# Moving the decay matrices and the first convolution tap to ScalarE, and all weight splits to VectorE, in a hybrid SSD and mLSTM layer

## The chip, the cores and the metric

The kernel runs on one core of a Trainium2 chip, as one program. The metric is the device time of one execution in microseconds (us), the median of several runs; lower is better. Engines are named as in the profile: PE is TensorE, DVE is VectorE, ACT is ScalarE, POOL is GpSimd, SP is SyncE, whose queue issues most DMAs.

## The reference, cut to what matters

One decoder layer for 1024 tokens of width 1024, all in float32. A normalised and modulated input `h` goes through one wide projection. Its columns feed a Mamba-2 branch (SSD: 32 heads in 4 groups, chunks of 128 tokens) and an mLSTM branch (4 heads); both merge, and a SwiGLU feed-forward follows. The change concerns the causal convolution that both branches begin with, and the decay matrices of the SSD branch:

```python
proj = h @ w_in[l]
z, xbc, dt, qk, v, o, if_pre, gate_pre = split_sizes(proj, IN_SPLITS)
...
xbc = jax.nn.silu(causal_depthwise_conv(xbc, conv_w, conv_b))     # 4 taps, per channel
...
a_cs = jnp.cumsum(a, axis=-1)                 # a = dt * A, per head and chunk
decay = jnp.exp(segsum(a))                    # exp(a_cs[l] - a_cs[s]) where l >= s, else 0
cb = jnp.einsum('bclgn,bcsgn->bgcls', cm, bm)
y_diag = jnp.einsum('bgcls,bgrcls,bcsgrp->bclgrp', cb, decay, x)
```

## The kernel before

All large products run on PE in exact pairs of float32r numbers: an operand is split into a high and a low part, and three matmuls (high by high, high by low, low by high) of 128 x 512 make one product. `split` (line 120) makes such a pair of a weight tile `raw` of 128 x 1024: ACT casts the high part `wh` (line 123), and another engine subtracts to get the low part `wl` (line 124). That engine is `eng["l"]`: POOL until the end of the SSD stage, DVE from there on (`eng["l"] = V`, line 677). There are two buffers of `wl` and three of `wh`, so a split waits until PE has finished with an older tile.

The work lies in stages. A prologue (about 0 to 60 us) loads `x`, normalises it and makes the modulation vectors, where DVE reduces 16 weight tiles (line 155). The SSD stage (about 60 to 600 us) does 16 head pairs, `ssd_pair`, four to a group. The mLSTM stage (about 600 to 1530 us) does four heads and the gates. Phase B (from about 1530 us) has the branch projections, the merge and the feed-forward.

`conv_tile` (line 293) makes one convolved tile of 128 channels x 1024 tokens: `gemm` fills a PSUM bank for each half (512 tokens) with 24 matmuls (line 287), ACT copies each to SBUF (`cr`, line 298), DVE makes the first tap and the bias out of `cr` (line 305) and adds three taps (line 307), ACT takes a tanh (line 308), and DVE finishes the SiLU (line 309). `gemm` has two banks (`mm`): PE fills one while the other is read.

`ssd_pair` (line 449) takes one `conv_tile`, and for each half `q` a tile `ab` of two heads by four chunks of 128 x 128: a DMA brings the cumulative sums along the row, POOL subtracts those of the column (line 466), DVE takes the minimum with 0 (line 467), ACT the exponential (line 468), DVE multiplies by the masked product of B and C (line 470), and PE multiplies by the values (line 494). `ab` has two buffers. `z_gate` (line 511) multiplies a result by silu(z): ACT takes the tanh from the bank (line 521), DVE multiplies it by the same bank (line 522), POOL does two more products (lines 523 and 533).

Within an engine, instructions run in the order of its queue. That order is not the order of the source: the framework's scheduler sets it at build time, from its own model of how long each instruction takes (`schedule_with_timeline_sim=True`). So a change of an instruction's engine also moves its neighbours.

Of the kernel before, what the change touches and what calls it, by code (L numbers as in the profile page):

```python
# [15 lines left out]
P = 128  # L16
# [3 lines left out]
NCH = 8  # L20
L = 128
# [15 lines left out]
def hybrid_layer(ctx: ExitStack, tc: tile.TileContext, a: dict, out: bass.AP, dbg=None):  # L37
# [80 lines left out]
    eng = {"l": G}  # L118

    def split(raw):  # L120
        wh = wp.tile([P, 1024], F32R, name="wh", bufs=NWH)
        wl = wp.tile([P, 1024], F32R, name="wl", bufs=NWL)
        A.copy(wh, raw)  # L123
        eng["l"].tensor_tensor(wl, raw, f(wh), SUB)  # L124
        return wh, wl
# [67 lines left out]
    def to_feat(src, bank, k, w, b, hf):  # L193
        """Four token-major tiles -> one modulated feature tile (128 x 512)."""
        for t in range(4):
            T.transpose(bank[:, t * P:(t + 1) * P], src[t][:, k * P:(k + 1) * P], ident)
        A.activation(hf, bank, AF.Identity, scale=mod[:, w, k:k + 1], bias=mod[:, b, k:k + 1])
# [5 lines left out]
    # =========================================================== norm 1 and the first products, k by k  # L203
# [12 lines left out]
    NG = 40                                                # dt (32), i (4), f (4)  # L216
# [75 lines left out]
    # ---- projection + causal conv + silu, feature-major  # L292
    def conv_tile(col, cw, cb, ti, pre=None):
        dst = xf("xf")
        cr = crt("cr")

        def epi(hf, ps):
            A.copy(cr[:, halves(hf)], ps)

        if pre is None:  # L300
            gemm(w_in[:, col:col + P], epi)
        else:
            for hf in range(2):
                epi(hf, pre[:, hf])
        V.tensor_scalar(dst, cr, cw[:, 3, ti:ti + 1], cb[:, ti:ti + 1], MUL, ADD)
        for sh in (1, 2, 3):
            V.scalar_tensor_tensor(dst[:, sh:], cr[:, :S - sh], cw[:, 3 - sh, ti:ti + 1], dst[:, sh:], MUL, ADD)  # L307
        A.activation(cr, dst, AF.Tanh)
        V.scalar_tensor_tensor(dst, cr, 1.0, dst, ADD, MUL)
        return dst  # L310
# [10 lines left out]
    # ---- per-token gates, token-major: columns dt (0..31), i (32..35), f (36..39) of every chunk  # L321
# [40 lines left out]
    V.scalar_tensor_tensor(flat(sp_), flat(gt), 0.0, flat(q0), MAX, ADD)      # softplus  # L362
    V.tensor_tensor(e0, sp_, fac.unsqueeze(1).broadcast_to([P, NCH, NG]), MUL)  # dt * A, log_f
    pcum, ptot = sc_bank()[:, 0:320], sc_bank()[:, 0:320]
    T.matmul(pcum, lhsT=mask01, rhs=flat(e0), start=True, stop=True)       # per-chunk cumulative sums
    T.matmul(ptot, lhsT=ones, rhs=flat(e0), start=True, stop=True)         # per-chunk totals on every partition
# [16 lines left out]
    # mLSTM stabilisers: rows of log_i - b, their running maximum, the maxima carried over chunks  # L383
# [29 lines left out]
    V.tensor_tensor(chv(cmx), chv(cmx), minb, MAX)          # mx = max(m_in, running max)  # L413
    V.tensor_tensor(chv(tw), minb, chv(cmx), SUB)           # w_inter = exp(m_in - mx)
# [6 lines left out]
    A.activation(em_t, em_t, AF.Exp, scale=-1.0)            # exp(-m_t), m_t = b + mx  # L421
# [3 lines left out]
    A.activation(w_t, w_t, AF.Exp)                          # exp(g - m_new + log_i - b)  # L425

    # ---- SSD
    sqacc = cp.tile([P, S], F32, name="sqacc")

    def ssd_bc(g):  # L430
        """C (feature-major), the masked products of B and C, and B token-major, for all chunks of a group."""
        b = conv_tile(OFF_B + P * g, cw_s, cb_s, 16 + g, pre=psb if g == 0 else None)
        cc = conv_tile(OFF_C + P * g, cw_s, cb_s, 20 + g)
        cbm, bt = xf("cbm"), xf("bt")
        for q in range(2):
            ps = sc_bank()
            for c in range(4):
                sl = slice((4 * q + c) * L, (4 * q + c + 1) * L)
                T.matmul(ps[:, c * L:(c + 1) * L], lhsT=b[:, sl], rhs=cc[:, sl], start=True, stop=True)
            V.tensor_tensor(cbm[:, halves(q)].rearrange("p (c l) -> p c l", l=L), ps.rearrange("p (c l) -> p c l", l=L),  # L440
                            mask01.unsqueeze(1).broadcast_to([P, 4, L]), MUL)
            ps = sc_bank()
            for c in range(4):
                sl = slice((4 * q + c) * L, (4 * q + c + 1) * L)
                T.transpose(ps[:, c * L:(c + 1) * L], b[:, sl], ident)
            A.copy(bt[:, halves(q)], ps)
        return cc, cbm, bt

    def ssd_pair(g, j, grp):
        """Heads 8g+2j and 8g+2j+1, all chunks; head pairs lie on partitions 0..63 and 64..127 of the result."""  # L450
# [11 lines left out]
        for q in range(2):  # L462
            ab[q] = ap.tile([P, 2, 4, L], F32, name="ab", tag="t4", bufs=2)
            Q.dma_start(ab[q].rearrange("p h c l -> p h (c l)"), acs_d[h0:h0 + 2, halves(q)].unsqueeze(0).broadcast_to([P, 2, 512]))
            ta = acs_t[:, 4 * q:4 * q + 4, h0:h0 + 2].rearrange("p c h -> p h c")
            G.tensor_tensor(ab[q], ab[q], ta.unsqueeze(3).broadcast_to([P, 2, 4, L]), SUB)  # L466
            V.tensor_scalar(ab[q], ab[q], 0.0, None, MIN)
            A.activation(ab[q], ab[q], AF.Exp)
# [42 lines left out]
    def z_gate(r, Y=None):  # L511
        """u = Y * silu(z) and its share of the row sums of squares; Y comes from DRAM where it was put off."""
# [22 lines left out]
    # ---- mLSTM  # L535
# [6 lines left out]
    def ml_v(h):  # L542
        """Token-major: tile i holds the 512 columns of the chunks 2i and 2i + 1."""
        vt = [xf("vt") for _ in range(4)]
        for u in range(2):
# [6 lines left out]
            for i in range(4):  # L552
                ps = mm_bank().rearrange("p (c n) -> p c n", c=2)
                for c in range(2):
                    sl = slice((2 * i + c) * L, (2 * i + c + 1) * L)
                    lo, hi = (0, 1, 2, 3), (4, 5, 6, 7)
                    if i + c == 0:                         # the low parts of the weights come last ...
                        order = ((0, 0, lo), (1, 0, lo), (0, 1, lo), (0, 0, hi), (1, 0, hi), (0, 1, hi))
                    else:                                  # ... and are given up first
                        order = ((0, 1, lo), (0, 1, hi), (0, 0, lo), (1, 0, lo), (0, 0, hi), (1, 0, hi))  # L560
                    ops = [(x_, w_, k) for x_, w_, ks in order for k in ks]
                    for n, (x_, w_, k) in enumerate(ops):
                        T.matmul(ps[:, c], lhsT=hT[k][x_][:, sl], rhs=ws[k // 4][w_][:, k % 4], start=n == 0, stop=n == 23)  # L563
# [11 lines left out]
    def ml_scan(h, q, k, v):  # L575
        C = ap.tile([P, 2, 514], F32, name="C")
        CH = CL = None
        for c in range(NCH):
# [37 lines left out]
            # state  # L616
# [26 lines left out]
            # normaliser, per-head rms  # L643
# [33 lines left out]
    eng["l"] = V  # L677
    later = chain(mod_steps(2, mod_row, 0), mod_steps(3, mod_cols, 2), mod_steps(4, mod_cols, 3), mod_steps(5, mod_row, 1))
    q, k, v = ml_q(0), ml_k(0), ml_v(0)
    def ssd_rms():  # L680
        # ssd rms: rows of 1/rms broadcast over partitions, times the factors left out above
# [35 lines left out]
    # =========================================================== phase B  # L717
# [30 lines left out]
    def kouter(nk, load, mm):  # L748
        """Products k by k into eight banks; the last two k bank by bank, so that the banks end one after another."""
# [9 lines left out]
    def residual(yt, ss, src, bk, ahead=None):  # L759
        """yt = src + two banks; ss = 1 / rms of its rows."""  # L760
# [201 lines left out]
```

## Time and profile before

| | |
|---|---|
| runs | 2756.96, 2765.63, 2765.8 us; median 2765.63 us |
| profiled execution: span from its first to its last instruction | 2757.1 us |
| PE busy | 2663.9 us, 97% of the span |
| DVE busy | 1449.5 us, 53% |
| ACT busy | 876.6 us, 32% |
| POOL busy | 657.4 us, 24% |

The page gives the profiled execution's own time by its span alone, which is as long as the shortest run; the median of the runs is 8.5 us above it. Busy shares are means over the whole span: the stages have different limits, so the rows below go by stage.

### The profile page before, as it was taken

How to read it: one execution, taken by the hardware profiler on the slowest of the kernel's cores; microseconds unless marked ns; L12 is line 12 of the kernel's file. 1: busy time of each engine (PE TensorE's matmuls, PEld its weight loads, DVE VectorE, ACT ScalarE, POOL GpSimd, SP SyncE). 2: the span in 40 equal slices, each digit the busy share in tenths (PEclk: the TensorE clock that was granted, in tenths of full speed). 3: DMA queues.
4: the chain of work that ended last, by engine and by line, in shares of the span. 5: the costliest groups of instructions: out<-in, count | busy, mean ns of one | idle time of the engine just before them, and what ended most of it. 6: DMA issues, size and time to landing. Idle time of an engine off the chain costs nothing.

```text
span 2757.1 us, 34111 instructions
## 1 busy us (share of the span) xinstructions
PE 2663.9 (97%) x13543; PEld 2223.4 (81%) x13543; DVE 1449.5 (53%) x2033; ACT 876.6 (32%) x1355; POOL 657.4 (24%) x447
## 2 busy tenths in 40 slices
PE   5999988999999999999999999999999999999998
PEld 3878777879888988988988877787788888788886
DVE  8688876895742463254354245536543343433333
ACT  5332322232431333243243223323242221322222
POOL 4333353420210011011032011401411134311154
PEclk9999999999999999999999999999999999999999
DMA  6323231343344332123132455646343333433332
GB/s 196 104 90 116 87 120 62 112 130 115 112 135 143 93 115 87 60 71 100 52 114 93 162 183 165 210 146 194 123 145 99 95 107 98 153 99 92 102 128 92
DMA packets 297000, 323.78 MB, mean 117 GB/s; under 512 B 15584, under 2 KB 224832, under 8 KB 296840
## 3 DMA queue, kind: packets, MB, share of 16 engines
q1 hardware_dynamic: 289416, 296.43, 34.8%
q0 software_dynamic: 7424, 25.17, 2.5%
q8 instruction: 106, 1.74, 0.3%
q14 instruction: 54, 0.44, 0.1%
HBM read 274.59 MB, written 46.96 MB: 117 GB/s over the span
## 4 chain that ended last, share of the span: by engine, by line
PE 74%; DVE 4%; DMA 1%; issue 1%; POOL 0%; ACT 0%; DVEq 0%; POOLq 0%; SPq 0%; ACTq 0%
PE mm L287 22%; PE mm L888 17%; PE mm L563 7%; PE n L800 6%; PE n L840 6%; PE mm L800 3%; PE sc L800 3%; PE mm L840 3%; PE sc L840 3%; PE n L615 2%; PE n L633 1%; DVE wl L124 1%; DMA uk<-y_d 1%; PE sc L584 1%; PE sc L655 1%
## 5 line engine op out<-in xcount | busy, mean ns | idle before, releaser
L124 DVE TENSOR_TENSOR wl<-raw,wh 128x1024 fp32r<-128x1024 f32 x283 | 395.7, 1400 | 665.8 <-issue 161.6
L123 ACT CAST wh<-raw 128x1024 fp32r<-128x1024 f32 x316 | 332.2, 1051 | 961.1 <-POOL raw L140 217.7
L287 PE MATMUL mm<-hh,wh 128*128 128x512 f32 x1392 | 551.1, 396 | 9.9 <-DVE tz L522 8.9
L287 PE MATMUL mm<-hl,wh 128*128 128x512 f32 x1392 | 550.3, 395 | 0.0
L287 PE MATMUL mm<-hh,wl 128*128 128x512 f32 x1392 | 548.0, 394 | 0.0
L888 PE MATMUL mm<-h,wh 128*128 128x512 f32 x1408 | 435.6, 390 | 2.1 <-DVE th L892 2.1
L287 PEld LDWEIGHTS mm<-hh,wh 128*128 128x128 f32 x1392 | 262.9, 189 | 65.2 <-DVE tz L522 9.9
L888 PEld LDWEIGHTS mm<-h,wh 128*128 128x128 f32 x1408 | 264.8, 188 | 57.3 <-DVE th L892 2.6
L287 PEld LDWEIGHTS mm<-hh,wl 128*128 128x128 f32 x1392 | 262.6, 189 | 52.0 <-issue 0.9
L287 PEld LDWEIGHTS mm<-hl,wh 128*128 128x128 f32 x1392 | 263.0, 189 | 50.3 <-issue 0.5
L888 PE MATMUL mm<-h,wl 128*128 128x512 f32 x704 | 274.9, 390 | 0.5 <-DVE wl L124 0.5
L140 POOL TENSOR_TENSOR raw<-raw,gb 128x1024 f32<-128x1024 f32 x60 | 151.9, 2533 | 305.1 <-DMA raw<-in_w_out_dram 175.0
L307 DVE SCALAR_TENSOR_TENSOR xf<-cr,pk,xf 128x1023 f32<-128x1023 f32 (+2 forms) x120 | 180.4, 1506 | 1.7
L800 PE MATMUL n<-us,wh 128*128 128x512 f32 x512 | 161.9, 397 | 2.8 <-DVE am L818 2.8
L896 POOL TENSOR_TENSOR act<-th,act 128x512 fp32r<-128x512 f32 x44 | 69.8, 1587 | 373.1 <-ACT act L895 373.1
L888 PEld LDWEIGHTS mm<-h,wl 128*128 128x128 f32 x704 | 132.5, 188 | 28.8 <-DVE wl L124 1.4
L124 POOL TENSOR_TENSOR wl<-raw,wh 128x1024 fp32r<-128x1024 f32 x33 | 89.4, 2710 | 174.4 <-PE mm L287 129.1
L191 POOL TENSOR_TENSOR sm<-sm,mhalf 128x1 f32<-128x1 f32 x32 | 20.2, 630 | 418.0 <-DVE sm L190 418.0
L800 PEld LDWEIGHTS n<-us,wh 128*128 128x128 f32 x512 | 96.8, 189 | 27.1 <-DVE am L818 3.3
L840 PE MATMUL n<-wh,act 128*128 128x512 f32 x352 | 116.7, 393 | 0.0
L466 POOL TENSOR_TENSOR ab<-ab,gsum 128x1024 f32<-128x1024 f32 x32 | 68.9, 2152 | 145.4 <-DMA ab<-acs_d 135.2
L800 PE MATMUL n<-us,wl 128*128 128x512 f32 x256 | 101.7, 399 | 0.0
(295 smaller groups left out, 4180.8 us busy)
## 6 DMA issues: line engine op xcount, KB each, us to landing
raw<-in_w_in_dram SPq DMA_DIRECT2D x104, 512.0 KB, 3.8
raw<-in_w_ffn_in_dram SPq DMA_DIRECT2D x88, 512.0 KB, 3.7
raw<-in_w_ffn_out_dram SPq DMA_DIRECT2D x44, 512.0 KB, 3.4
raw<-in_w_ada_dram SPq DMA_DIRECT2D x40, 512.0 KB, 3.7
tg_d<-tz POOLq DMA_DIRECT2D x64, 256.0 KB, 2.9
ab<-acs_d SPq DMA_DIRECT2D x32, 512.0 KB, 3.8
raw<-in_w_branch_ssd_dram SPq DMA_DIRECT2D x32, 512.0 KB, 3.6
tgl<-tg_d SPq DMA_DIRECT2D x64, 256.0 KB, 2.9
```

Source lines behind the costliest of these rows:

```text
L123: A.copy(wh, raw)
L124: eng["l"].tensor_tensor(wl, raw, f(wh), SUB)
L140: G.tensor_tensor(raw, raw, gate, MUL)
L287: T.matmul(ps, lhsT=ww[:, k, :], rhs=xx[:, halves(hf)], start=n == 0, stop=n == 23)
L307: V.scalar_tensor_tensor(dst[:, sh:], cr[:, :S - sh], cw[:, 3 - sh, ti:ti + 1], dst[:, sh:], MUL, ADD)
L466: G.tensor_tensor(ab[q], ab[q], ta.unsqueeze(3).broadcast_to([P, 2, 4, L]), SUB)
L563: T.matmul(ps[:, c], lhsT=hT[k][x_][:, sl], rhs=ws[k // 4][w_][:, k % 4], start=n == 0, stop=n == 23)
L615: T.matmul(nv(i), lhsT=l_, rhs=r_, start=n == 0, stop=n == len(ops) - 1)
L800: T.matmul(bk[j], lhsT=l_[:, js], rhs=us[:, r_], start=first and n == 0, stop=last and n == 2)
L840: T.matmul(bk[i], lhsT=at[:, l_, tt * P:(tt + 1) * P], rhs=r_[:, halves(nh)], start=first and n == 0, stop=last and n == 2)
L888: T.matmul(ps, lhsT=ww[:, k, :], rhs=h2[k][:, r_], start=k == 0 and n == 0, stop=k == KD - 1 and n == 2)
L896: G.tensor_tensor(at[:, 1], th, f(at[:, 0]), SUB)
```

## The change

Three edits. The first: the low part of every weight split is made by DVE, in the prologue and the SSD stage too. The second: the first tap of a convolution, with its bias, is made by ACT straight from the PSUM bank, half by half, where DVE made it of the copy. The third: for the decay matrices, POOL's subtraction and DVE's minimum become one ACT function with a column of biases, `relu(t - a)` for each block of 128 x 128 (the column's sum t is one number for each partition), and the exponential is taken of its negative: exp(-max(t - a, 0)) = exp(min(a - t, 0)).

```diff
-    eng = {"l": G}
-
     def split(raw):
...
         A.copy(wh, raw)
-        eng["l"].tensor_tensor(wl, raw, f(wh), SUB)
+        V.tensor_tensor(wl, raw, f(wh), SUB)
         return wh, wl
...
         def epi(hf, ps):
             A.copy(cr[:, halves(hf)], ps)
+            A.activation(dst[:, halves(hf)], ps, AF.Identity, scale=cw[:, 3, ti:ti + 1], bias=cb[:, ti:ti + 1])
...
-        V.tensor_scalar(dst, cr, cw[:, 3, ti:ti + 1], cb[:, ti:ti + 1], MUL, ADD)
...
-            ta = acs_t[:, 4 * q:4 * q + 4, h0:h0 + 2].rearrange("p c h -> p h c")
-            G.tensor_tensor(ab[q], ab[q], ta.unsqueeze(3).broadcast_to([P, 2, 4, L]), SUB)
-            V.tensor_scalar(ab[q], ab[q], 0.0, None, MIN)
-            A.activation(ab[q], ab[q], AF.Exp)
+            for e in range(2):
+                for c in range(4):
+                    A.activation(ab[q][:, e, c], ab[q][:, e, c], AF.Relu, scale=-1.0, bias=acs_t[:, 4 * q + c, h0 + e:h0 + e + 1])
+            A.activation(ab[q], ab[q], AF.Exp, scale=-1.0)
...
-    eng["l"] = V
```

The rest of the diff takes out comments, so lines of the changed kernel stand two lower from `split` on and three lower from the end of the SSD stage on.

What becomes of the order on POOL: in the SSD stage of the kernel before, POOL's queue holds weight splits (L124) and subtractions of decay tiles (L466) between the products of `z_gate` (L523, L533).

```order
L124 TENSOR_TENSOR wl<-raw,wh 128x1024
L466 TENSOR_TENSOR ab<-ab,gsum 128x1024 x2
L523 TENSOR_TENSOR Y<-Y,tz 128x512 x2
L124 TENSOR_TENSOR wl<-raw,wh 128x1024
L533 TENSOR_TENSOR sqacc<-sqacc,sq 128x512 x2
L124 TENSOR_TENSOR wl<-raw,wh 128x1024
```

In the changed kernel the same stretch holds those products alone (L521 and L531 are L523 and L533 of before).

```order
L314 DMA tg_d<-tz 128x512 x4
L521 TENSOR_TENSOR Y<-Y,tz 128x512 x4
L531 TENSOR_TENSOR sqacc<-sqacc,sq 128x512 x2
L521 TENSOR_TENSOR Y<-Y,tz 128x512 x2
L531 TENSOR_TENSOR sqacc<-sqacc,sq 128x512 x2
```

Every split and every subtraction has left POOL's queue.

On ACT, this is the first head pair in the kernel before: copies of banks (L298), the first copy of a state (L484), a weight cast (L123), a copy of a result (L503) and one exponential of a decay tile (L468).

```order
L484 COPY st<-n_1123 128x128
L123 CAST wh<-raw 128x1024
L298 COPY cr<-mm 128x512
L503 COPY Y<-n_1146 128x128
L468 ACTIVATE ab<-ab 128x1024
L298 COPY cr<-mm 128x512
```

The same place in the changed kernel (L296 is the copy of a bank, L297 the first tap, L465 the relu, L466 the exponential):

```order
L482 COPY st<-n_1138 128x128
L465 ACTIVATE ab<-ab,gsum 128x128 x8
L121 CAST wh<-raw 128x1024
L296 COPY cr<-mm 128x512
L297 ACTIVATE xf<-mm,pk_105 128x512
L466 ACTIVATE ab<-ab 128x1024
L501 COPY Y<-n_1161 128x128
L465 ACTIVATE ab<-ab,gsum 128x128 x8
L296 COPY cr<-mm 128x512
L297 ACTIVATE xf<-mm,pk_105 128x512
```

Eight small instructions now stand ahead of an exponential, and here the copy of a bank stands right behind them.

On DVE, this is the end of the SSD stage's first pair in the kernel before: mask products of decay tiles (L470), a minimum (L467), the skip term (L504), the end of a SiLU (L309), steps of the states (L488) and a first tap (L305).

```order
L470 TENSOR_TENSOR ab<-ab,cbm 128x1024
L467 TENSOR_SCALAR ab<-ab 128x1024
L504 SCALAR_TENSOR_TENSOR Y<-xf,dskip,Y 128x1024
L309 SCALAR_TENSOR_TENSOR xf<-cr,xf 128x1024
L488 SCALAR_TENSOR_TENSOR st<-st,ecb,n_1345 128x64 x2
L470 TENSOR_TENSOR ab<-ab,cbm 128x1024
L488 SCALAR_TENSOR_TENSOR st<-st,ecb,n_1345 128x64 x7
L305 TENSOR_SCALAR xf<-cr,pk_105 128x1024
```

The same place in the changed kernel (L468 is the mask product, L307 the end of the SiLU, L122 the split, L305 the three later taps, L474 and L476 two scaled copies of the values):

```order
L468 TENSOR_TENSOR ab<-ab,cbm 128x1024
L307 SCALAR_TENSOR_TENSOR xf<-cr,xf 128x1024
L122 TENSOR_TENSOR wl<-raw,wh 128x1024
L305 SCALAR_TENSOR_TENSOR xf<-cr,pk_105,xf 128x1023
L305 SCALAR_TENSOR_TENSOR xf<-cr,pk_105,xf 128x1022
L305 SCALAR_TENSOR_TENSOR xf<-cr,pk_105,xf 128x1021
L474 TENSOR_TENSOR xd<-sc,gsum 128x512
L476 TENSOR_TENSOR xe<-sc,gsum 128x512
```

The split stands among them, ahead of the taps; the minimum and the first tap are gone.

## Rows read from the trace of the kernel before

**Rows 1.** Busy us (count) by stage: PE, PEld, DVE, ACT, POOL; then granted clock.

```profile
60.00:600.00 540.00, 508.97 (x2833) 416.90 (x2832) 436.14 (x572) 159.44 (x229) 203.76 (x96) 0.97 0.32 101
600.00:1530.00 930.00, 927.47 (x5420) 814.97 (x5419) 445.77 (x867) 328.58 (x570) 121.12 (x146) 1.00 0.33 102
```

**Rows 2.** Waits of PE in 60 to 600 us: total us, times, longest us.

```profile
PE mm L287 <- DVE tz L522: 8.9, 3, 8.0
PE n L481 <- DVE xe L478: 6.9, 5, 2.3
PE sc L439 <- DVE xf L309: 5.9, 2, 4.4
PE sc L473 <- DVE xf L309: 3.2, 3, 1.4
PE mm L287 <- ACT cr L298: 1.0, 2, 0.6
```

**Rows 3.** Timeline around the longest of them: start us, us, idle before.

```profile
407.52 4.45 POOL L533 TENSOR_TENSOR sqacc<-sqacc,sq 128x512 f32<-128x512 f32 x2
...
410.77 5.55 DVE L307 SCALAR_TENSOR_TENSOR xf<-cr,pk,xf 128x1022 f32<-128x1022 f32 x2
...
416.98 0.80 PE L287 MATMUL mm<-hh,wh 128*128 128x512 f32 x1 [7.99 <-DVE tz L522]
...
417.57 0.63 PE L287 MATMUL mm<-hl,wh 128*128 128x512 f32 x1
```

**Rows 4.** Groups of DVE, 60 to 600 us: busy us, mean ns, idle before.

```profile
L307 DVE SCALAR_TENSOR_TENSOR xf<-cr,pk,xf 128x1023 f32<-128x1023 f32 (+2 forms) x72 | 117.4, 1634 | 1.0
L470 DVE TENSOR_TENSOR ab<-ab,cbm 128x1024 f32<-128x1024 f32 x30 | 44.0, 1466 | 8.3 <-ACT ab L468 8.3
L309 DVE SCALAR_TENSOR_TENSOR xf<-cr,xf 128x1024 f32<-128x1024 f32 x24 | 38.5, 1604 | 11.0 <-ACT cr L308 10.8
L305 DVE TENSOR_SCALAR xf<-cr,pk 128x1024 f32<-128x1024 f32 x25 | 37.9, 1520 | 5.6 <-ACT cr L298 5.6
...
L467 DVE TENSOR_SCALAR ab<-ab 128x1024 f32<-128x1024 f32 x30 | 26.4, 880 | 15.5 <-POOL ab L466 15.5
```

**Rows 5.** The same groups in the mLSTM stage, 600 to 1530 us.

```profile
L124 DVE TENSOR_TENSOR wl<-raw,wh 128x1024 fp32r<-128x1024 f32 x69 | 85.6, 1241 | 220.0 <-PE mm L287 116.4 <-PE mm L563 82.4 <-ACT wh L123 21.1
...
L307 DVE SCALAR_TENSOR_TENSOR xf<-cr,pk,xf 128x1023 f32<-128x1023 f32 (+2 forms) x48 | 63.1, 1314 | 0.7
L309 DVE SCALAR_TENSOR_TENSOR xf<-cr,xf 128x1024 f32<-128x1024 f32 x16 | 20.1, 1255 | 9.7 <-ACT cr L308 9.7
...
L470 DVE TENSOR_TENSOR ab<-ab,cbm 128x1024 f32<-128x1024 f32 x2 | 2.4, 1214 | 0.0
```

**Rows 6.** Groups of POOL, 60 to 600 us.

```profile
L124 POOL TENSOR_TENSOR wl<-raw,wh 128x1024 fp32r<-128x1024 f32 x32 | 87.1, 2722 | 174.4 <-PE mm L287 129.1 <-issue 29.1 <-ACT cr L308 10.6
L466 POOL TENSOR_TENSOR ab<-ab,gsum 128x1024 f32<-128x1024 f32 x30 | 64.3, 2142 | 116.5 <-DMA ab<-acs_d 106.4 <-DVE ab L470 7.9 <-ACT sm L408 2.2
```

**Rows 7.** Groups of ACT, 0 to 130 us: operations with per-partition operands.

```profile
L153 ACT ACTIVATE modraw<-modraw,cact 128x128 f32<-128x128 f32 x64 | 19.5, 389 | 11.3 <-DMA modraw<-in_w_ada_dram 11.3
L197 ACT ACTIVATE hf<-mm,mod 128x512 f32<-128x512 f32 x16 | 11.9, 770 | 14.4 <-DVE hl L201 7.3 <-PE mm L196 2.9 <-PE sc L103 2.4
```

**Rows 8.** Groups of ACT, 60 to 600 us.

```profile
L468 ACT ACTIVATE ab<-ab 128x1024 f32<-128x1024 f32 x30 | 31.8, 1060 | 79.5 <-DVE ab L467 78.1 <-issue 1.4
L298 ACT COPY cr<-mm 128x512 f32<-128x512 f32 x49 | 28.3, 578 | 37.7 <-PE mm L287 37.6
```

**Rows 9.** Timeline of the prologue, where POOL's first split runs.

```profile
23.27 0.75 DVE L237 TENSOR_SCALAR xx<-xx,rs 128x1024 f32<-128x1024 f32 x1 [0.44 <-POOL rs L191]
...
24.68 2.35 POOL L124 TENSOR_TENSOR wl<-raw,wh 128x1024 fp32r<-128x1024 f32 x1
24.75 2.83 DVE L237 TENSOR_SCALAR xx<-xx,rs 128x1024 f32<-128x1024 f32 x1 [0.66 <-POOL rs L191]
```

**Rows 10.** The chain that ended last, its longest unbroken piece before 900 us.

```profile
829.38 54.69 PE mm L287 x240
```

## The prediction

> **What bounds the kernel now.** I read the busy times by stage first. In the mLSTM stage PE is busy 927.47 of 930 us, so nothing that is moved there between the other engines can give time, as long as PE is still fed. In the SSD stage, 60 to 600 us, PE is busy 508.97 of 540 us: 31.0 us idle. DVE is busy 436.14 us there (81%), ACT 159.44 us (30%), POOL 203.76 us (38%) [rows 1]. So PE's work sets the end almost everywhere, and what this change can touch is above all those 31 us.
>
> Then I asked the waits of PE what those 31 us are: 8.9 + 6.9 + 5.9 + 3.2 = 24.9 us are waits for DVE, and 1.0 us for a copy on ACT [rows 2]. The stage is short of DVE, in bursts; ACT has room.
>
> The timeline shows how the longest wait, 8.0 us, comes about. POOL does two products for 4.45 us, and meanwhile and afterwards two taps on DVE take 5.55 us. Behind them in DVE's queue stands `tz` (line 522), the second reader of a bank of `gemm`; PE waits 7.99 us for that bank and starts at 416.98 us [rows 3]. A tap takes 1314 ns in the mLSTM stage [rows 5], so here two took 2.78 us each: DVE is slow while POOL runs. The groups say the same of the whole stage: 1634 ns a tap, 1604 for the end of a SiLU and 1466 for a mask product [rows 4], against 1314, 1255 and 1214 later [rows 5].
>
> **What each part costs.** First DVE, in the SSD stage. Removed: the minima, 26.4 us, and the first taps, 37.9 us [rows 4]. Added: POOL's 32 splits [rows 6] at 1241 ns, DVE's own price for one in the next stage [rows 5]: 39.7 us. POOL loses 87.1 + 64.3 = 151.4 us of work [rows 6] out of 203.8 [rows 1], 74%. What POOL's running costs DVE is, for the three groups that stay, 72 x 0.320 + 24 x 0.349 + 30 x 0.252 = 39.0 us [rows 4, 5]; 74% of that is 28.9 us. So DVE goes by -26.4 - 37.9 + 39.7 - 28.9 = -53.5 us, to about 383 us of 540 (71%).
>
> The Trainium skill (SBUF — State Buffer, section "Who interferes with whom") says that DVE and GpSimd share one pair of ports, which whoever issues first holds for its whole instruction, while the other is blocked fully. By that reading alone DVE would win back up to 81% of the 151.4 us, some 123 us, and not 29: an estimate from the Trainium skill's rule and rows of this case. The stretch that I can see in the groups is 39 us in all, so I keep the rows' 28.9; the larger figure would speak for the first rival below.
>
> ACT, in the same stage: 30 decay tiles x 8 relus. The trace has the same shape with one per-partition operand, in runs of eight: 64 in 19.5 us, 305 ns each [rows 7], so 240 x 0.305 = 73.2 us. The first taps: 49 halves [rows 8] at 770 ns, the price of the one operation with scale and bias columns out of a bank [rows 7], 37.7 us. ACT goes from 159 to 270 us, 50% of the stage. By throughput it is covered: PE's 509 us hide it. A block on ACT from relu to exponential is 2.44 + 1.06 us [rows 7, 8]. With copy and first tap (0.58 + 0.77) behind it, a bank is held for 4.85 us. PE needs 240 matmuls in 54.69 us [rows 10], so 24 x 0.228 = 5.47 us for the other bank; with everything in place it does not wait. If that cover of 0.62 us is gone, each us more is a us of PE.
>
> The chain of a decay tile gets shorter in hand-overs: DMA, ACT, DVE, PE, where it was DMA, POOL, DVE, ACT, DVE, PE. The 78.1 us that ACT's queue stood still for the minimum [rows 8] go, and with them what was held up behind. What can be late next is the DMA itself, seen from ACT.
>
> In the mLSTM stage DVE loses 15 first taps and ACT gains 30 at 0.77 us, 23 us on top of 329 of 930; PE idles there 2.5 us [rows 1], so I price it at nothing, with PE's own work as the cover. Phase B has no edited operation: its splits were on DVE already. There is one table load on ACT in either order, so relu and identity bring no switch.
>
> In the prologue the one split on POOL (2.35 us) held a scaling on DVE for 2.83 us, where the one before it took 0.75 [rows 9]. On DVE the two cost 0.75 + 1.24 = 1.99 us: -0.8 us, on the engine that the prologue waits for.
>
> The sum on the path, for the PE waits. The 8.9 us on `tz` go whole, since POOL's split and the first tap that crowded them are gone. Of the other 16.0 us on DVE I take half, 8.0: DVE's load falls by an eighth, its queue is still in order, and the split now stands ahead of taps. Those two are choices; the bounds are 0 and 24.9. Then the clock: right after the 8 us stall a matmul takes 0.63 us [rows 3], at the lower of the two levels, 1.2 GHz. The stage's mean of 0.97 bounds this at 0.03 x 540 = 16 us [rows 1], but much of that lies in idle time itself; I choose 1.5 us, near the low end. Against it stand new waits on ACT. Today they are 1.0 us at 159 us of work; I allow 4 us, by choice, for 270 us with blocks of 3.5 us in them. Sum: -8.9 - 8.0 - 1.5 - 0.8 + 4 = -15.2 us. The profiled span of 2757.1 us becomes 2742, and the median of the runs, 2765.6, becomes 2750.
>
> **The rivals.** Less than 0.3% (8.3 us) of change is what a measurement of this kernel can hardly tell from none.
>
> *All of it (16%).* PE's idle time in the stage goes to nearly nothing: 31.0 + 1.5 of clock + 0.8 = 33, so 2732. For it: every long wait was DVE's, and DVE is relieved. Against it: the queues are in order and newly planned, and a plan never fits all.
>
> *No change, by the splits (26%).* In the mLSTM stage, where DVE has the splits, each of 69 waits (116.4 + 82.4) / 69 = 2.9 us for PE to give a buffer of `wl` free [rows 5]; POOL had such waits too, 129.1 us [rows 6], where nobody stood behind it. On DVE, taps and scaled copies stand behind it. 32 x 2.9 = 93 us on top of 383 makes 476. DVE's other idle time, 540 - 436 = 104, less the 15.5 for POOL's subtraction [rows 4], adds 88: 564 of 540, and the stage is full again. Then the 31 us stay, and the time is 2766, give or take 8. Against it: DVE idled anyway in the mLSTM stage, so its waits there may be mere early arrival.
>
> *Slower, by ACT (16%).* POOL waited 106.4 us over 30 decay tiles for their DMA, 3.5 us each [rows 6]. Now ACT stands at that DMA, with copies of banks behind it. In the changed order 14 of 32 blocks have a reader of `gemm`'s bank at most two rows behind. A wait of w costs 14 x (w - 0.62) us: 40 us at w = 3.5, which makes 2791 with the rest as forecast. It is slower by over 8.3 us from w = 2.3 on. Against it: POOL was often at the head of its queue because it had nothing else, and the scheduler puts the relu where it expects the data to be there.
>
> The Trainium skill (ScalarE: Activation LUTs, "Rules for kernel authors") tells to do relu, min and add on VectorE, not on ScalarE; that speaks against the third edit. In engine time the rows agree: 2.44 us of relus for one minimum of 0.88 us [rows 4, 7].
>
> **How the numbers follow.** The forecast, 2750, has 42%, for times from about 2742 to 2757. Faster by over 0.3% are it and the first rival, less a little for its upper edge: 0.57. No change: 0.27. Slower: 0.16. For eight in ten I go from 2729, just under the first rival, to 2776, which takes in the whole of "no change" and ACT's wait up to about w = 2.4 us; what is left out is the longer ACT waits and some of the first rival.
>
> **What would show it.** Right, if in 60 to 600 us DVE's busy time falls by some 50 us and a tap costs near 1.4 us, ACT's rises to about 270, POOL's falls to about 50, and PE's waits on `tz`, `xe` and `xf` sum to under 10 us, with those on ACT under 5. The forecast is wrong if the split on DVE has long waits with PE waiting for `xf` or `xe` behind it; or if PE waits on the copy, on the first tap or on `tz` while ACT's relus wait for the DMA of the decay tile; or if a scheduler's new order moves waits into the mLSTM stage, where PE now has almost none.

## The result and the profile after

The changed kernel takes 2745.18 us, the median of four runs (2744.59 to 2748.33); the kernel before, run beside it, takes 2762.9 (2756.96 to 2765.8). The ratio is 0.9936, 95% interval [0.9918, 0.9953]: 17.7 us faster. The span of the profiled execution is 2742.7 us, where 2742 was forecast; for the median of the runs 2750 was forecast.

Engine by engine, the page of the changed kernel says (busy us, share of the span, instructions):

```profile
PE 2660.2 (97%) x13543; PEld 2220.5 (81%) x13543; DVE 1381.0 (50%) x1994; ACT 1004.8 (37%) x1691; POOL 501.7 (18%) x382
```

PE has the same 13543 instructions. Its busy time falls by 3.7 us (2663.9 before) and its idle time by 10.7: 2757.1 - 2663.9 = 93.2 before, 2742.7 - 2660.2 = 82.5 after. The two make the 14.4 us of the span.

By stage, the two rows that answer to [rows 1]:

```profile
60.00:600.00 540.00, 522.45 (x2951) 430.60 (x2950) 393.03 (x577) 273.81 (x545) 61.80 (x34) 0.99 0.35 106
600.00:1530.00 930.00, 926.37 (x5381) 812.68 (x5381) 417.52 (x826) 346.22 (x597) 114.46 (x145) 1.00 0.34 101
```

In the SSD stage PE idles 17.55 us, where it idled 31.0. The mLSTM stage stays full. Phase B gives a little back: PE's waits for `wl` at the merge and feed-forward (line 837) are 9.7 us in six, 6.7 in five before.

The waits of PE in the SSD stage, which answer to [rows 2]:

```profile
PE sc L471 <- DVE xf L307: 7.4, 2, 3.9
PE mm L285 <- ACT xf L297: 4.3, 1, 4.3
PE sc L437 <- DVE xf L307: 2.1, 1, 2.1
PE sc L437 <- DVE cbm L438: 1.8, 3, 0.9
```

The waits on `tz` and `xe` are gone. Those on `xf`, the convolved tile that DVE finishes late, are as long as before in total: 7.4 + 2.1 = 9.5 us, where they were 5.9 + 3.2 = 9.1. And there is a new one: PE waits 4.3 us for a bank that ACT's first tap (line 297) still reads.

The groups of DVE in this stage, which answer to [rows 4], and the splits that it has taken over:

```profile
L305 DVE SCALAR_TENSOR_TENSOR xf<-cr,pk,xf 128x1023 f32<-128x1023 f32 (+2 forms) x78 | 108.4, 1392 | 14.5 <-ACT xf L297 13.9
L122 DVE TENSOR_TENSOR wl<-raw,wh 128x1024 fp32r<-128x1024 f32 x36 | 45.1, 1252 | 22.2 <-PE mm L285 13.9 <-PE n L254 4.4 <-DMA u_d<-Y 2.5
L468 DVE TENSOR_TENSOR ab<-ab,cbm 128x1024 f32<-128x1024 f32 x31 | 40.5, 1308 | 15.2 <-ACT ab L466 15.1
L307 DVE SCALAR_TENSOR_TENSOR xf<-cr,xf 128x1024 f32<-128x1024 f32 x25 | 33.5, 1339 | 18.7 <-ACT cr L306 18.7
```

A tap costs 1392 ns instead of 1634. The splits wait 22.2 us, not the 93 us of the second rival. But DVE now stands 13.9 us for ACT's first tap.

On ACT, the relus and the first taps in the same stage:

```profile
L465 ACT ACTIVATE ab<-ab,gsum 128x128 f32<-128x128 f32 x256 | 78.4, 389 | 85.5 <-DMA ab<-acs_d 78.4 <-PE n L496 6.6 <-PE mm L285 0.5
L297 ACT ACTIVATE xf<-mm,pk 128x512 f32<-128x512 f32 x51 | 39.6, 783 | 0.0
```

The relus go at 78.4 / 256 = 306 ns (305 forecast), the taps cost 783 ns (770 forecast). ACT stands 78.4 us for the DMA of the decay tiles, as the third rival said, and PE does not follow: apart from the 4.3 us above it waits 0.8 us for ACT, 0.6 of them on a weight cast and 0.2 on a copy of a result.

The new wait, in the timeline of ACT and PE:

```profile
83.00 0.58 ACT L296 COPY cr<-mm 128x512 f32<-128x512 f32 x1
...
87.55 0.47 ACT L345 ACTIVATE e<-gt 128x320 f32<-128x320 f32 x1 [3.97 <-DVE gt L344]
...
87.98 1.04 ACT L121 CAST wh<-raw 128x1024 fp32r<-128x1024 f32 x1
...
88.93 0.58 ACT L296 COPY cr<-mm 128x512 f32<-128x512 f32 x1
...
89.78 0.77 ACT L297 ACTIVATE xf<-n,pk 128x512 f32<-128x512 f32 x1
90.44 0.58 ACT L296 COPY cr<-n 128x512 f32<-128x512 f32 x1
90.91 0.80 ACT L297 ACTIVATE xf<-n,pk 128x512 f32<-128x512 f32 x1
91.58 1.46 ACT L297 ACTIVATE xf<-mm,pk 128x512 f32<-128x512 f32 x2
92.43 0.79 PE L285 MATMUL mm<-hh,wh 128*128 128x512 f32 x1 [4.30 <-ACT xf L297]
...
96.36 0.40 PE L285 MATMUL mm<-hh,wh 128*128 128x512 f32 x1
```

PE has filled both banks by 88.13 us (92.43 - 4.30). The copy of the first was done at 83.58, and with one reader that bank would be free from then on. Its first tap starts at 91.58: the scheduler had put it behind a gate's exponential, for which ACT stood 3.97 us, a weight cast, the other bank's copy, a second function of the gates, and a copy and two taps of another tile. So the bank is held until PE starts at 92.43, 8.8 us longer than by its copy. This is the worst case and not the rule: of the 51 first taps in the stage 43 start right behind the copy of their bank, and eight start 1.2 to 8.0 us after its end. When PE begins at 92.43, its clock has fallen, as windows of 2 us show (the last three columns are granted clock, DMA share and GB/s):

```profile
92.00:94.00 2.00, 1.57 (x4) 1.29 (x5) 1.86 (x5) 1.05 (x2) 0.00 (x0) 0.50 0.30 91
94.00:96.00 2.00, 2.00 (x6) 1.52 (x5) 1.93 (x4) 0.00 (x0) 0.00 (x0) 0.50 0.00 0
96.00:98.00 2.00, 2.00 (x10) 1.64 (x9) 2.00 (x3) 0.00 (x0) 0.00 (x0) 0.94 0.00 0
```

After the 4.30 us of idling the granted clock is 0.50, which is 1.2 GHz. Nine matmuls start in 96.36 - 92.43 = 3.93 us; at the 0.228 us each of [rows 10] they take 2.05. So this one wait costs 4.3 + 1.9 = 6.2 us.

### The profile page after: what moved, and what is told of

Its sections match the earlier page's. It is cut to its first block, busy times and chain, and to the rows that moved or that the text cites. A ratio compares the mean times of both kernels' runs of the same rounds, so it can differ in the third digit from the quotient of the medians.

```text
span 2742.7 us, 34287 instructions
## 1 busy us (share of the span) xinstructions
PE 2660.2 (97%) x13543; PEld 2220.5 (81%) x13543; DVE 1381.0 (50%) x1994; ACT 1004.8 (37%) x1691; POOL 501.7 (18%) x382
## 4 chain that ended last, share of the span: by engine, by line
PE 85%; DVE 6%; DMA 4%; ACT 2%; issue 2%; POOL 1%; SPq 0%; DVEq 0%; POOLq 0%; ACTq 0%
PE mm L285 30%; PE mm L885 17%; PE mm L561 7%; PE n L797 6%; PE n L837 5%; PE mm L797 3%; PE sc L797 3%; PE mm L837 3%; PE sc L837 3%; PE n L613 2%; DMA ab<-acs_d 1%; PE n L631 1%; DVE wl L122 1%; PE n L492 1%; ACT ab L465 1%
## 5 line engine op out<-in xcount | busy, mean ns | idle before, releaser
L122 DVE TENSOR_TENSOR wl<-raw,wh 128x1024 fp32r<-128x1024 f32 x316 | 441.0, 1397 | 697.4 <-issue 160.7
L305 DVE SCALAR_TENSOR_TENSOR xf<-cr,pk,xf 128x1023 f32<-128x1023 f32 (+2 forms) x120 | 162.2, 1353 | 23.8 <-ACT xf L297 22.7
L465 ACT ACTIVATE ab<-ab,gsum 128x128 f32<-128x128 f32 x256 | 78.4, 389 | 85.5 <-DMA ab<-acs_d 78.4
L189 POOL TENSOR_TENSOR sm<-sm,mhalf 128x1 f32<-128x1 f32 x32 | 17.7, 554 | 479.8 <-DVE sm L188 479.8
L521 POOL TENSOR_TENSOR Y<-Y,tz 128x512 f32<-128x512 f32 x14 | 33.4, 2404 | 384.9 <-DVE Y L502 221.7
```

The source lines that it names most:

```text
L122: V.tensor_tensor(wl, raw, f(wh), SUB)
L465: A.activation(ab[q][:, e, c], ab[q][:, e, c], AF.Relu, scale=-1.0, bias=acs_t[:, 4 * q + c, h0 + e:h0 + e + 1])
```

## The experiments

The change has three edits; below, "split", "tap" and "decay". Three theories, A to C, stood at the start; D and E came after the first group of five runs. A: POOL's long two-input operations stretch DVE's, and what counts is the work that leaves POOL. B: the length of DVE's own list counts. C: the scheduler's new order gives or takes some 10 us at random. D: the first tap on ACT costs time, whatever the other edits. E: it costs only as long as ACT also waits for DVE's minimum. Times are medians; each stands beside runs of the kernel before on its own chip (2761.2, 2761.18 and 2761.55 us in the three groups of runs; 2762.9 beside the changed kernel).

### Each edit alone

`only_split`: the kernel before, with

```diff
-        eng["l"].tensor_tensor(wl, raw, f(wh), SUB)
+        V.tensor_tensor(wl, raw, f(wh), SUB)
```

> The kernel before with the first edit alone: all weight splits on DVE, taps and decay tiles as before. Theory A (POOL's long operations stretch DVE's, so what counts is the work that leaves POOL): POOL loses 87 of 204 us in the SSD stage, a tap falls from 1634 to about 1500 ns, DVE's busy time grows by about 23 us, and PE's idle time of 31 us falls by some 5 us; 3 to 8 us faster than before. Theory B (what counts is DVE's own load): DVE has 40 us more to do, PE's idle time grows; 5 to 10 us slower. Theory C (the scheduler's new plan decides): anything within 10 us either way, without a relation to a tap's length.

2749.5 us, ratio 0.9957 [0.9944, 0.9971]: 11.7 us faster. PE idles 23.7 us in the SSD stage, a tap costs 1437 ns. DVE is 15 us busier there (451.6), and yet the kernel is faster: B does not fit, and A has the sign but with 3 to 8 us not the size.

`only_tap`: the kernel before, with

```diff
+            A.activation(dst[:, halves(hf)], ps, AF.Identity, scale=cw[:, 3, ti:ti + 1], bias=cb[:, ti:ti + 1])
...
-        V.tensor_scalar(dst, cr, cw[:, 3, ti:ti + 1], cb[:, ti:ti + 1], MUL, ADD)
```

> The kernel before with the second edit alone: first tap on ACT out of the bank. Theory A: POOL stays as it is, a tap stays near 1630 ns, time within 3 us of before. Theory B: DVE loses 38 us in the SSD stage, the larger part of the 64 us that the change takes off it; 8 to 12 us faster. Theory C: within 10 us either way.

2779.82 us, 1.0072 [1.0059, 1.0086]: 18.6 us slower, though DVE has lost 25 first taps. None of the three theories had this. The exponential's group on ACT:

```profile
L468 ACT ACTIVATE ab<-ab 128x1024 f32<-128x1024 f32 x28 | 29.7, 1060 | 112.2 <-DVE ab L467 112.2
```

ACT now stands 112.2 us for the minimum (78.1 in [rows 8]), and PE idles 44.5 us, 6.6 of them at the first tap.

`only_decay`: the kernel before, with the eight relus and the exponential in place of the subtraction and the minimum, as in the change's diff.

> The kernel before with the third edit alone: decay tiles by relu on ACT. Theory A: POOL loses 64 us, a tap falls to about 1530 ns; 5 to 10 us faster. Theory B: DVE loses 26 us; 4 to 7 us faster. Both agree here in sign; the length of a tap and the waits of PE tell how it comes. Theory C: within 10 us either way.

2730.96 us, 0.9887 [0.9873, 0.9902]: 30.2 us faster, more than the whole change and three times the most that A had for it. The SSD stage:

```profile
60.00:600.00 540.00, 528.26 (x3000) 435.02 (x2999) 413.81 (x587) 243.37 (x498) 129.30 (x66) 1.00 0.35 108
```

PE idles 11.7 us there.

### Work put on POOL

`pool_load`: the changed kernel, with two additions of the convolved tile to the running sum of squares on POOL, at each of two places of each head pair but the first. The sum is then no longer the layer's.

```diff
+        for _ in range(2 if r else 0):
+            G.tensor_tensor(sqacc, sqacc, xs, ADD)
```

> The changed kernel with work put back on POOL that nothing waits for: in each head pair but the first, four additions of the convolved tile to the running sum of squares, 60 operations of 128 x 1024 with two inputs, about 130 us. The sum is then not the layer's. Theory A: a tap rises from 1392 to about 1600 ns, PE's idle time in the SSD stage rises from 17.6 us to nearly 30, and the time is 10 to 17 us above the changed kernel, so near the kernel before. Theory B: DVE's list of instructions is unchanged, the time is within 3 us of the changed kernel. Theory C: within 10 us either way.

2794.89 us, 1.012 [1.0104, 1.0137]: 49.7 us above the changed kernel. The SSD stage:

```profile
60.00:600.00 540.00, 501.76 (x2737) 412.26 (x2738) 403.85 (x528) 253.45 (x500) 201.34 (x84) 0.96 0.31 96
```

The later taps on DVE there, and one half of the additions:

```profile
L305 DVE SCALAR_TENSOR_TENSOR xf<-cr,pk,xf 128x1023 f32<-128x1023 f32 (+2 forms) x72 | 126.7, 1762 | 12.1 <-ACT xf L297 11.4
...
L454 POOL TENSOR_TENSOR sqacc<-sqacc,xf 128x1024 f32<-128x1024 f32 x26 | 72.9, 2804 | 88.8 <-DVE xf L307 84.8 <-DVE st L490 1.6 <-ACT sqacc L530 1.2
```

POOL is as busy as before the change, a tap is longer than before the change, and PE's idle time (38.2 us) is worse than the 31.0 of [rows 1]. The sign is A's, the size is not: A had 10 to 17 us. PE waits there above all for DVE: for `xf` 16.5 us in total, for `xe` 8.1 and for the states 3.7. Over the whole span its 13543 instructions are busy 17.4 us longer than in the changed kernel; the mean granted clock of the stage is 0.96.

### Pairs of edits, and a longer list for DVE

`no_tap`: split and decay; in the changed kernel

```diff
-            A.activation(dst[:, halves(hf)], ps, AF.Identity, scale=cw[:, 3, ti:ti + 1], bias=cb[:, ti:ti + 1])
...
+        V.tensor_scalar(dst, cr, cw[:, 3, ti:ti + 1], cb[:, ti:ti + 1], MUL, ADD)
```

> The changed kernel with the first tap back on DVE, so the first and third edits alone. Theory D (a first tap on ACT makes DVE's taps and the bank wait for whatever ACT's queue waits for, and costs time in every company): 8 to 20 us faster than the changed kernel, near 2730 us; no wait of PE on a first tap, and DVE's taps wait for nobody. Theory E (that cost came only of ACT standing still for the minimum, which the third edit takes away): within 4 us of the changed kernel. If the three edits simply added up, it would be the runs alone, -12 and -30 us, so 2719; PE's idle time of 12 us left in the SSD stage of the third edit alone says that not all of this is there to be had.

2724.26 us, 0.9864 [0.985, 0.9877]: 36.9 us faster than before, 20.9 faster than the changed kernel, and the fastest of all that were run, by 1 us. Its SSD stage:

```profile
60.00:600.00 540.00, 532.87 (x3016) 440.07 (x3015) 427.39 (x633) 244.86 (x501) 57.21 (x34) 0.99 0.35 108
```

The waits of PE there, without those on the norm and the prologue's sums:

```profile
PE n L479 <- DVE xe L476: 3.8, 3, 2.4
...
PE sc L471 <- DVE xf L307: 0.9, 1, 0.9
```

Its first taps on DVE:

```profile
L303 DVE TENSOR_SCALAR xf<-cr,pk 128x1024 f32<-128x1024 f32 x27 | 25.1, 931 | 5.9 <-ACT cr L296 5.5
```

DVE is busier than in the changed kernel (427 us for 393), and PE idles only 7.1 us. A first tap on DVE costs 931 ns here, not the 1520 of [rows 4].

`no_split`: tap and decay; in the changed kernel the split goes back to POOL.

```diff
-        V.tensor_tensor(wl, raw, f(wh), SUB)
+        eng["l"].tensor_tensor(wl, raw, f(wh), SUB)
```

> The changed kernel with the splits back on POOL, so the second and third edits alone. Added up from the runs alone: +19 and -30, so 2750 us, 5 us above the changed kernel. Theory A (POOL stretches DVE): a tap on DVE is longer than 1392 ns, near 1450 as POOL has 82 us more. Theory E: the first tap costs nothing here, so it is near the third edit alone, 2731 us.

2746.26 us, 0.9941 [0.9929, 0.9954]: 1 us from the changed kernel.

`no_decay`: split and tap; the changed kernel with POOL's subtraction and DVE's minimum of before.

> The changed kernel with the decay tiles back on POOL and DVE, so the first and second edits alone. Added up: -12 and +19, so 2768 us. Theories D and E both expect the first tap to cost here, as ACT still waits for the minimum: ACT's wait for it stays over 60 us, and PE waits on first taps, taps and mask products behind it. If the time is below 2755 instead, the cost of the first tap came of POOL's splits.

2759.98 us, 0.9994 [0.9984, 1.0004]: nothing is left of the gain. PE's waits on ACT's first tap are 8.1 us, the longest 4.3.

`dve_load`: the changed kernel with two one-input operations more on DVE at the end of each head pair.

```diff
+        for _ in range(2):
+            V.tensor_scalar(Y, Y, -1e30, None, MAX)
```

> The changed kernel with two operations more on DVE in each head pair, a maximum with -1e30 of the result tile in place, which changes nothing: 32 of some 0.7 us, 22 us of DVE, which nobody on PE waits for. It takes back nearly the net 25 us by which the edits shorten DVE's list. Theory B (DVE's list counts): 8 us or more slower than the changed kernel. Theory A (POOL's company counts): within 5 us of it.

2744.89 us, 0.9938 [0.9924, 0.9951]: no difference, with 19 us more of DVE in the stage (412.4). Here B does not hold, and a plan with 32 instructions more does not move the time, which speaks against C.

So the first tap on ACT costs 18.6 us alone, 10.5 beside split (2759.98 - 2749.5), 15.3 beside decay (2746.26 - 2730.96) and 20.9 beside both. D holds. E falls: without the minimum on DVE the tap costs 15.3 and 20.9 us, with it 18.6 and 10.5.

### What the first tap costs by, and what POOL's work does

Four last runs. F: the first tap costs by ACT's load in an in-order queue. G: by what hangs on it, the bank's second reader or the DVE taps that wait for it.

`act_load`: `no_tap`, with ScalarE work that nobody on PE's path waits for.

```diff
+        for _ in range(2):
+            A.copy(Y, Y)
```

> The version with the first and third edit alone (first tap on VectorE, 2724 us) plus 32 ScalarE copies of the result tile Y (128 x 1024) onto itself, after the skip term; at 1.06 us, the price of an exponential of that size, some 34 us more on ScalarE in the SSD stage, about what the first taps bring (39.6 us), on no chain that PE waits for. The result is unchanged. Theory F (the first tap costs by ScalarE's load and its in-order queue: other copies and tanhs come late): 15 to 20 us slower than 2724, near 2742, and VectorE's waits for ScalarE's tanh and state copies rise from 9.4 and 14.1 us towards the 18.7 and 25.7 of the changed kernel. Theory G (it costs by what hangs on the tap itself, the bank's second reader or the three taps behind it): within 5 us of 2724.

2725.29 us, 0.9868 [0.9855, 0.9882]: 1 us from `no_tap`. Its SSD stage:

```profile
60.00:600.00 540.00, 532.53 (x3015) 440.79 (x3016) 423.62 (x626) 273.00 (x529) 52.14 (x34) 0.99 0.35 108
```

ACT is busy 273.0 us, as in the changed kernel (273.81), and PE idles 7.5 us instead of 17.55. F falls, as far as load at this place of the queue can tell.

`tap_sbuf`: the changed kernel with the first tap still on ACT, but out of the copy.

```diff
-            A.activation(dst[:, halves(hf)], ps, AF.Identity, scale=cw[:, 3, ti:ti + 1], bias=cb[:, ti:ti + 1])
...
+        A.activation(dst, cr, AF.Identity, scale=cw[:, 3, ti:ti + 1], bias=cb[:, ti:ti + 1])
```

> The changed kernel, but ScalarE makes the first tap out of the SBUF copy in one operation of 128 x 1024, behind the second copy, so the bank is free after the copy; ScalarE's work falls a little (two operations of 0.78 us become one of about 1.1). If holding the bank for a second reader is what the first tap costs: most of the 21 us come back, near 2728. If it is ScalarE's load, or that VectorE's taps must wait for ScalarE (theories F and the dependency half of G): within 5 us of 2745, and VectorE's wait for the first tap stays near 14 us.

2731.21 us, 0.9892 [0.9879, 0.9906]: 14.0 of the 20.9 us are back. The SSD stage:

```profile
60.00:600.00 540.00, 531.30 (x3021) 439.55 (x3022) 407.60 (x606) 273.44 (x526) 57.94 (x34) 0.99 0.35 109
```

The later taps on DVE:

```profile
L305 DVE SCALAR_TENSOR_TENSOR xf<-cr,pk,xf 128x1023 f32<-128x1023 f32 (+2 forms) x81 | 112.3, 1388 | 22.7 <-ACT xf L303 22.2
```

DVE waits longer for ACT's tap than in the changed kernel (22.2 us, 13.9 there), ACT is as busy, and yet PE idles only 8.7 us. So neither ACT's load nor DVE's waiting for ACT is the larger part. The bank is what is left, but this is argued and not isolated, since the edit moves two things besides it: the tap is one operation instead of two, and the scheduler made a new order. Against the order speaks that three other new orders, `dve_load`, `pool_memset` and `act_load`, stand within 1 us of the kernels they were made from.

`pool_memset`: as `pool_load`, but POOL writes constants and reads nothing.

```diff
+        for _ in range(3 if r else 0):
+            G.memset(sqacc, 1.0)
```

> The changed kernel plus 90 GpSimd fills of one SBUF tile with a constant (128 x 1024, six for each head pair but the first; the tile is the sum of squares, which is then no longer the layer's). GpSimd is busy as in the run with 60 two-input operations (201 us there) or near it, but reads nothing. Theory A in the narrow form (it is GpSimd's reading, the shared port, that stretches VectorE): a tap stays within 1.38 to 1.45 us, and the time within 10 us of 2745, what it is above coming of the products that queue behind the fills. Theory A in the wide form (any work on GpSimd): a tap near 1.7 us and the time near 2785 to 2795.

2744.79 us, 0.9938 [0.9924, 0.9951]: no difference from the changed kernel. The later taps, and one half of the fills:

```profile
L305 DVE SCALAR_TENSOR_TENSOR xf<-cr,pk,xf 128x1023 f32<-128x1023 f32 (+2 forms) x78 | 106.2, 1364 | 13.1 <-ACT xf L297 12.5
...
L454 POOL MEMSET sqacc<- 128x1024 f32 x45 | 43.0, 955 | 3.7 <-ACT sqacc L530 1.2
```

The fills came out shorter than expected: POOL is busy 144.7 us in the stage, not 201. With 86 us of fills a tap is 28 ns shorter than in the changed kernel; with 143.7 us of additions it is 370 ns longer. The timelines say it tap by tap. In both runs a later tap with nothing on POOL beside it takes 1.27 to 1.29 us. Of those that ran for more than half their time beside the new work alone, 22 beside fills took 1.27 to 1.29 us and 17 beside additions 1.9 to 3.5. POOL's reading stretches DVE; its writing does not.

`decay_dve`: `no_tap` with subtraction and minimum of a block in one DVE operation.

```diff
-                    A.activation(ab[q][:, e, c], ab[q][:, e, c], AF.Relu, scale=-1.0, bias=acs_t[:, 4 * q + c, h0 + e:h0 + e + 1])
-            A.activation(ab[q], ab[q], AF.Exp, scale=-1.0)
+                    V.tensor_scalar(ab[q][:, e, c], ab[q][:, e, c], acs_t[:, 4 * q + c, h0 + e:h0 + e + 1], 0.0, SUB, MIN)
+            A.activation(ab[q], ab[q], AF.Exp)
```

> The version with the first and third edit alone (2724 us), but the subtraction and minimum of a decay tile are eight VectorE operations of 128 x 128 (subtract the column, minimum with 0) in place of ScalarE's eight relus; the exponential stays on ScalarE. At 0.284 us, the row of a 128 x 128 operation of this kind elsewhere in this kernel, 256 of them are 73 us more on VectorE (427 to some 500 of 540 us) and 78 less on ScalarE. Theory H (VectorE's list is then the bound of the stage): 10 to 25 us slower than 2724, PE's waits on xf and xe over 20 us. Theory B denied (VectorE's list still does not count, as with 22 us more in an earlier run): within 5 us of 2724. The Trainium skill (ScalarE: Activation LUTs, Rules for kernel authors) tells to put relu and min on VectorE: by it this is no slower, or faster.

2735.62 us, 0.9906 [0.9892, 0.9919]: 11.4 us slower than `no_tap`. The SSD stage:

```profile
60.00:600.00 540.00, 524.26 (x2932) 433.81 (x2932) 456.25 (x837) 167.53 (x237) 58.95 (x34) 0.98 0.34 104
```

The group of the new operations on DVE:

```profile
L465 DVE TENSOR_SCALAR ab<-ab,gsum 128x128 f32<-128x128 f32 x240 | 55.9, 299 | 10.5 <-DMA ab<-acs_d 10.3
```

DVE is busy 456 us and PE idles 15.7. Theory H, that DVE's list is then the bound of the stage, holds at its lower end, though the new operations took 55.9 us and not the 73 expected, and not by the waits that it named: those on `xf` and `xe` are under 1 us, and those on `tz`, on the states and on a copy of a result took their place (4.9, 4.2 and 4.3 us). The rule of the Trainium skill (ScalarE: Activation LUTs, "Rules for kernel authors") to put relu and min on VectorE does not hold here as advice on where to put them. By engine time it does: 55.9 us for 240 on DVE are 233 ns each, where ACT takes 306.

## Why the prediction came out right, and where it did not

**The span.** The forecast was -15.2 us, the span fell by 14.4. The terms, as measured in the changed kernel: the waits on `tz` were to lose 8.9 us and did. The other 16.0 us of waits on DVE were to lose 8.0 and lost 6.5: the 6.9 on `xe` whole, while those on `xf` grew by 0.4. New waits on ACT were allowed 4 us; they are 4.3 + 0.8 instead of 1.0, so 4.1. These three terms were to give 12.9 us and gave 11.3. The stage's idle time fell by 13.5; the rest are small waits that had no term (those on `tkm` and `red` lose 2.8 us, those on `cbm` gain 1.1). The clock was to give 1.5 us and the prologue 0.8; PE's busy time fell by 3.7, and it idles 26.2 us of the first 60 where it idled 27.5. Behind 600 us PE idles some 4 us more than before (13.5 + 1.3 - 10.7), which no term had. Of the prediction's signs, those on DVE (43 us less), on a tap (1392 ns), on ACT, on POOL and on the waits for `tz`, `xe` and `xf` (9.5 us) came; the waits on ACT are 5.1 us where it had under 5, and one of the signs against it came in part: PE waits on the first tap, but behind a gate and not behind a relu.

**DVE.** Right in kind and near in size: 393 us, 383 forecast. POOL's work in the stage fell by 70% (74% forecast). The stretch of a tap fell by (1634 - 1392) / (1634 - 1314) = 76%, that of the end of a SiLU by 76% and that of a mask product by 63%, against 74%. That this stretch is POOL's doing was argued in the prediction; `pool_load` now shows it. In [rows 3] the two products end before the second of the two taps begins; what ran beside that one is a split that stands between the rows shown:

```profile
411.93 3.32 POOL L124 TENSOR_TENSOR wl<-raw,wh 128x1024 fp32r<-128x1024 f32 x1
```

One point was open: whether POOL's full time or only the seen stretch counts. The Trainium skill (SBUF — State Buffer, "Who interferes with whom") says that a DVE instruction with two SBUF inputs contends with a GpSimd instruction that reads SBUF, and not with one that only writes; the trace agrees, with 1762 ns for a tap beside additions and 1364 beside fills.

**The mis-sized term** is the first tap. The prediction counted its 37.9 us on DVE as gain, and its price on the path as part of the 4 us for ACT. `no_tap` shows that the edit costs 20.9 us, and that without it the other two give 36.9. So the 17.7 us are a gain of 36.9 and a loss of 20.9, less what noise there is in the runs (the two sums differ by 1.7 us), and the forecast came near their difference by luck: its sum had neither in full. The step that failed is the sentence on the bank: 0.58 us of copy and 0.77 of tap behind a block of 3.5 us make 4.85 of 5.47 us, "with everything in place it does not wait". At 88 us not everything was in place: between a bank's copy and its tap stood a wait for DVE and work on another tile, and no relu. A wait on the first tap of 4.3 us at the longest stands in all seven kernels of this study that make it out of PSUM, each time between 88 and 96 us, and in none of the others. It explains 6.2 of the 20.9 us. The profiled executions of the changed kernel and `no_tap` are 20.0 us apart: PE idles 10.4 us more in the SSD stage and 3.5 more elsewhere, and the same 13543 instructions are busy 6.1 us longer, as the matmuls behind the wait at 92.43 are. In the stage the larger waits that differ are the 4.3 us on the tap and those on late `xf`, 9.5 us for 0.9; against them stand 3.8 us on `xe` that only `no_tap` has. `tap_sbuf` shows that 14.0 come back when the tap does not hold the bank; its waits on `xf` are 3.4 us. How a bank that is held makes `xf` late was not shown. The last 7 us, between `tap_sbuf` (2728.74 to 2736.88 in four runs) and `no_tap`, may be DVE's wait for ACT's tap or the order; that stays open.

One late `xf` can be followed in the timeline:

```profile
366.75 1.28 DVE L305 SCALAR_TENSOR_TENSOR xf<-cr,pk,xf 128x1022 f32<-128x1022 f32 x1
366.97 5.58 POOL L521 TENSOR_TENSOR Y<-Y,tz 128x512 f32<-128x512 f32 x2 [66.27 <-DVE Y L502]
...
369.08 2.33 DVE L305 SCALAR_TENSOR_TENSOR xf<-cr,pk,xf 128x1021 f32<-128x1021 f32 x1
...
372.57 0.63 ACT L530 ACTIVATE sq<-Y 128x512 f32<-128x512 f32 x1 [1.59 <-POOL Y L521]
373.11 1.04 ACT L306 ACTIVATE cr<-xf 128x1024 f32<-128x1024 f32 x1
...
376.13 1.11 PE L471 MATMUL sc<-ident,xf 128*128 128x128 f32 x4 [3.91 <-DVE xf L307]
```

Two things meet. The last tap takes 2.33 us beside POOL's products. The one before began 0.22 us ahead of them and took 1.28 us, as it does alone, though POOL ran beside it for the rest. The last tap ends at 371.41, but the tanh of the tile stands on ACT behind a square that waits for POOL, and starts at 373.11. PE waits 3.91 us at the end of it.

**The rivals.** "No change, by the splits" fell: the splits on DVE wait 22.2 us and not 93, and `only_split` is 11.7 us faster. "Slower, by ACT" had its mechanism (78.4 us at the DMA, 2.9 us for each of 27 waits) without its price: PE waits on ACT at no decay tile. "All of it" names the size that the change has without the tap: 2724 where it said 2732.

**The decay edit** carries the gain: 30.2 us alone. The prediction's sum gave it no term of its own. POOL is left with 129.3 us of work in `only_decay` and with 125.3 in `only_split`, which gains 11.7. So some 18 of the 30 us are not POOL's relief, if the splits that `only_split` adds to DVE cost nothing themselves; `dve_load` makes that likely and does not show it. What is left is the minimum that leaves DVE and the hand-over that is gone. `decay_dve` keeps both operations off POOL, but it brings the hand-over from DVE to ACT back (ACT stands 60.9 us for it) and 55.9 us of work on DVE; it loses 11.4 us. How the gain divides between the two was not tried.

## What to carry to other kernels

A second reader of a PSUM bank is priced by where the scheduler may put it, not by its own duration: if it does not stand right behind the first reader, the bank is held for all that stands between, so let one reader copy and work on from SBUF; here that gave back 14.0 of 20.9 us. Where several edits come together, run each alone and each left out: here two good ones hid a bad one of more than half their size. Relieving the busiest helper engine was worth little here for its own sake: `no_tap` has 34 us more on DVE in the SSD stage than the changed kernel and is 20.9 us faster. What counts is whose result PE waits for, and which engine's reads run beside it.

## What the hardware showed that was not expected

- A group's mean hides two kinds of operations. With nothing on POOL beside it, a first tap out of SBUF takes 0.81 us and a later tap 1.28, in the kernel before as in `no_tap`. Where POOL ran beside it for more than half its time, they took 1.92 and 2.63 us on average in the kernel before. So both lose over a microsecond each time, and the first tap's mean falls further (1520 ns [rows 4] to 931, where a later tap goes from 1634 to 1323) above all because 16 of 25 first taps ran so, and 19 of 72 later taps.
- A POOL fill of 128 x 1024 takes 955 ns and leaves a tap on DVE at its 1.28 us; an addition of that size takes 2804 ns in the group shown and stretches it.
- PE's clock: after 4.30 us of idling the rows show 0.50 for the next 3.9 us, so that the wait cost nearly half as much again.
